# Compact S5 weights in scratch memory, a second rotation table, and a delay before preparation products in the recorded list

## The chip, the cores and the metric

One core of one Trainium2 chip runs the whole program in one launch. The metric is the device time of an execution in microseconds (us). Each of the core's engines follows its own list of instructions in order: PE is TensorE's matmul, PEld its weight load, DVE is VectorE, ACT is ScalarE, POOL is GpSimd, SP is SyncE, which here only issues DMAs. A wait of one instruction holds up everything behind it on its engine.

## The reference, cut to what matters

The reference is eleven stages on 256 tokens of width 1024: gated feed-forward layers, an S5 mixer, three attention mixers, two squared-relu layers and a final norm. The change concerns the first feed-forward layer (`ffn0`), beside which the S5 weights are prepared, and the S5 mixer behind it.

```python
h = h + 0.5 * swiglu(rms_norm(h, g0), w_gate, w_up, w_down)   # ffn0
hn = rms_norm(h, mix_norm)
u = hn @ w_in                                                  # S5
dt = exp(log_dt); lam = exp(a * dt)                            # complex, 64 groups x 64 states
bb = (lam - 1) / a * b
state[t] = lam * state[t - 1] + bb @ u[t]                      # per group of 16 channels
y = real(c @ state) + d * u
g = gelu(y); g = g * sigmoid(g @ w_glu); h = h + g @ w_out
```

## The kernel before, in words

**Lists.** The kernel is recorded as operations with their tiles. A scheduler (`Schedule.run`) plays them with fixed prices and writes one list for each engine. An operation has a class: `HEAD`, `CRIT`, `FILL`, `LATE` and, last, `BACK`, which is taken only when nothing else can run. All of S5's preparation is `BACK`, so it is woven between the work of `ffn0`. The play decides only the order; on the chip each engine runs its list with semaphore waits. DMAs are issued from SP and from ACT in list order, and share eight completion semaphores in turn: a ninth DMA waits on its own engine until the first has landed. Every instruction is emitted at line L519.

**Weights.** A 128x1024 piece `raw` is loaded by SP, rounded by ACT to `whi`, and DVE forms the rest `wlo` (6, 6 and 5 buffers). PE multiplies both with the activations (`xs` or `hid`).

**Start.** `load_x` loads the eight feature tiles of `x` into `h`, the first of them from ACT's queue, and `table` makes ACT load its function table early with a one-column activation on `ident`. PE fills the start with ten products of `ident` with itself.

**Preparation** (`s5_prep`). After a chain of small DVE operations it makes, for each half of the 32 pairs of groups, a table of rotations in one buffer `tb` (`table`), and for each of eight tiles m: input weights (`enter`, DVE, then four ACT copies with a mask into `et`), output weights (`powers`, DVE into `pg`, then two ACT copies into `gz`), and products of `gz` with the input matrix `bz` on PE, which give the short lags (`tile_mats`). Two groups share 128 partitions, so `et`, `gz` and the lags hold zeros where one group's channels meet the other's states. Each part goes by a DMA of its own into the DRAM scratch `s5_dr[m]`, 2688 columns wide; the rotations too.

**S5** (`s5`). `load(m)` brings `s5_dr[m]` back into `mt` (two of four buffers lie in `hid`, the room of ffn0's hidden layer, which is free when ffn0's last product is done). `state(m)` multiplies with `et` on PE, DVE rotates, scans and rotates back, `outy(m)` multiplies with the lags and `gz`, and ACT applies gelu. Products with `w_s5i` (`umm`) and `w_s5g` (`glu`) stand between.

```python
        def load(m):
            mts[m] = mbuf[m % 4]
            D.dma_start(out=mts[m], in_=self.s5_dr[m])
```

Of the kernel before, what the change touches and what calls it, by code (L numbers as in the profile page):

```python
# [15 lines left out]
AF = mybir.ActivationFunctionType  # L16
# [15 lines left out]
MT = 2688  # L32
# [142 lines left out]
class Recorder:  # L175
# [71 lines left out]
    def add(self, calls, cls):  # L247
# [5 lines left out]
        o.lat = 2.0 if o.dma else 0.0  # L253
# [29 lines left out]
class Schedule:  # L283
# [6 lines left out]
    def run(self):  # L290
# [106 lines left out]
        while True:  # L397
# [40 lines left out]
            for what, o in batch:  # L438
# [4 lines left out]
                else:  # L443
# [8 lines left out]
                    for b in succ[o]:  # L452
                        if o.wkind is not None and o.wkind == b.wkind:
                            lat = 0.0
                        elif o.eng == b.eng and (not o.dma or b.dma):
                            lat = o.lat if b.eng in "PD" else self.rec.SAME
                        else:
                            lat = self.rec.CROSS + o.lat
                        b.at = max(b.at, now + lat)
                        left[b] -= 1  # L460
                        if not left[b]:
                            if b.at > now + 1e-9:
                                push(b.at, "wake", b)
                            else:
                                avail_add(b)
# [58 lines left out]
class Net:  # L524
# [351 lines left out]
    def s5_prep(self):  # L876
# [9 lines left out]
        self.s5_dn = keep("s5_dn", [P, KD])  # L886
        self.s5_dr = [self.sb(f"s5_dr{m}", [P, MT], pool="dram") for m in range(KD)]
# [111 lines left out]
        tb = tmp("tb", [P, 2, 16, 64])  # L999
# [43 lines left out]
        mask = tmp("mask", [P, 2])  # L1043
        D.dma_start(out=mask, in_=A["s5_mask"])
        bt = tb.rearrange("p r j c -> p (r j c)")[:, 0:1024].rearrange("p (m r c) -> p m r c", m=KD, r=2)
        lbs = [pb.rearrange("p r j n -> p (r j n)").rearrange("p (m s r c) -> p m s r c", m=2, s=4, r=2), tmp("lb", [P, 2, 4, 2, 64])]
        gzs = [tmp(f"gz{i}", [P, 2, 4, 4, 32]) for i in range(2)]
        ets = [tmp(f"et{i}", [P, 4, 2, P]) for i in range(2)]
        lags = [tmp(f"lag{i}", [P, P]) for i in range(2)]
# [5 lines left out]
        for z in gzs + [bz]:  # L1055
            G.memset(z, 0.0)

        def table(half):

            j0 = 16 * half  # L1060
            G.memset(tb[:, 0, :, 31:32], 1.0)
# [30 lines left out]
        def enter(m):  # L1092
# [6 lines left out]
            tt(V, a[:, 0], a[:, 0], b[:, 1], SUB)  # L1099
            tt(V, a[:, 1], a[:, 1], b[:, 0], ADD)  # L1100
            et = ets[m % 2]
            for g in range(2):
                for r in range(2):
                    S.activation(et[:, :, r, 64 * g:64 * g + 64], a[:, r], AF.Copy, scale=mask[:, g:g + 1])
            S.dma_start(out=self.s5_dr[m][:, 0:1024], in_=et.rearrange("p s r q -> p (s r q)"))

        def powers(m):
# [4 lines left out]
            gz = gzs[m % 2]  # L1112
# [4 lines left out]
            tt(V, pa, pa, pq, SUB)  # L1117
            for g in range(2):
                ps = slice(64 * g, 64 * g + 64)
                S.activation(gz[ps].rearrange("p r s j (g n) -> p (r s j) g n", g=2)[:, :, g, :],  # L1120
                             pa[ps].rearrange("p q j n -> p (q j) n"), AF.Copy)

        def tile_mats(m):
# [5 lines left out]
            gz = gzs[m % 2]  # L1129
            S.dma_start(out=self.s5_dr[m][:, 1024:2048], in_=gz.rearrange("p r s j q -> p (r s j q)"))  # L1130
# [6 lines left out]
            V.scalar_tensor_tensor(p[:, 0:32], i4, self.s5_dn[:, m:m + 1], p[:, 0:32], op0=MUL, op1=ADD)  # L1137
            S.activation(lags[m % 2], p[:, 0:P], AF.Copy)
            S.dma_start(out=self.s5_dr[m][:, 2048:2176], in_=lags[m % 2])
# [10 lines left out]
    def s5(self, ph, nxt):  # L1150
# [7 lines left out]
        def share(shape):  # L1158
# [5 lines left out]
            names = "abc"[:len(shape)]  # L1164
# [10 lines left out]
        for t in zss + m4s:  # L1175
            G.memset(t, 0.0)
# [8 lines left out]

        def scale(m):
# [4 lines left out]
        def state(m):  # L1191
            u, mt = us[m], mts[m]
            et = mt[:, 0:1024].rearrange("p (s r q) -> p s r q", s=4, r=2)
            ps = [self.ps(b)[:, 0:P].rearrange("p (r c) -> p r c", r=2) for b in sbanks]
            with self.r.group(CRIT):
                for ri in range(2):
                    for s in range(4):
                        for j in range(4):
                            a = slice(32 * j, 32 * j + 32)
                            PE.matmul(ps[j][:, ri, :], lhsT=et[a, s, ri, :], rhs=u[a, s, :], start=s == 0, stop=s == 3,  # L1200
# [3 lines left out]
            tab = mt[:, 2176:MT].rearrange("p (e j c) -> p e j c", e=2, j=4)  # L1204
# [10 lines left out]
            for ri in range(2):  # L1215
# [3 lines left out]
                            mt[:, 2176:MT].rearrange("p (e q) -> p e q", e=2).unsqueeze(2).to_broadcast([P, 2, 2, T]), op=MUL)  # L1219
# [5 lines left out]
        def outy(m):  # L1225
            z, u, mt = zss[m % NZ], us[m], mts[m]
            gz = mt[:, 1024:2048].rearrange("p (r s j q) -> p r s j q", r=2, s=4, j=4)
            ps = self.ps(4)[:, 0:T].rearrange("p (s c) -> p s c", s=4)
            with self.r.group(CRIT):
                for d in range(4):  # L1230
                    for j in range(4):
                        a = slice(32 * j, 32 * j + 32)
                        PE.matmul(ps[a, d:4, :], lhsT=mt[a, 2048 + 32 * d:2080 + 32 * d], rhs=u[a, 0:4 - d, :], start=d == 0, stop=False,
# [749 lines left out]
```

## Time and profile before

| | us |
|---|---|
| median of 3 runs | 1579.7 (1579.31 to 1580.79) |
| profiled execution | 1576.88 |
| its span, first to last instruction | 1575.1 |
| PE busy | 1538.8 |
| DVE, ACT, POOL busy | 1177.5, 946.3, 76.2 |

The profiled execution is the one in which all rows were taken; it took 1.8 us beside its span, and 2.8 us less than the median. Busy times of engines overlap, so they don't add up. A busy PE can be a slow PE: the column PEclk gives the granted clock, 1.00 for 2.4 GHz and 0.50 for 1.2 GHz, and a mean between them says how a stretch is divided. The S5 preparation runs from about 45 to 230 us, ffn0 ends and S5 begins at about 218 us, and S5 ends near 340 us.

### The profile page before, as it was taken

The page shows a single profiled execution, that of the slowest core. Times are in us where ns is not written, and L with a number is a line of the kernel's source. Part 1 is how long each engine was busy: PE and PEld are TensorE (multiplying, and loading weights), DVE is VectorE, ACT ScalarE, POOL GpSimd, SP SyncE. Part 2 cuts the span into 40 slices and gives each one's busy share as a digit, 9 for nine tenths or more (in the row PEclk, how much of TensorE's full clock was granted, in tenths as well). Part 3 has the DMA queues.
Part 4 walks back from the last instruction along what each step waited for, and adds up shares of the span by engine and source line. Part 5 has one row for each costly group of instructions (what it writes and reads, how often), then busy time and mean ns, then how long its engine had stood idle before and what let it go on. Part 6 is the DMA issues. An engine that isn't in the chain of part 4 may idle for free.

```text
span 1575.1 us, 28813 instructions
## 1 busy us (share of the span) xinstructions
PE 1538.8 (98%) x11018; PEld 1383.7 (88%) x11018; DVE 1177.5 (75%) x2205; ACT 946.3 (60%) x1800; POOL 76.2 (5%) x111
## 2 busy tenths in 40 slices
PE   8998998999999999999999999999999999999998
PEld 8998887998888888889998888989888888888887
DVE  5997878877777777767878777797876557787663
ACT  6566662466655566645666665565787447688642
POOL 1000000000000000003310000010000002100000
PEclk8999999999999999999999999999999999999999
DMA  7667887356656555655447666632665542356561
GB/s 255 216 195 266 255 307 275 133 187 189 187 185 189 184 185 188 187 163 164 134 161 226 188 186 188 207 116 90 217 203 187 188 143 78 122 178 211 186 189 40
DMA packets 94682, 289.29 MB, mean 184 GB/s; under 512 B 18768, under 2 KB 23760, under 8 KB 93520
## 3 DMA queue, kind: packets, MB, share of 16 engines
q1 hardware_dynamic: 90224, 277.44, 55.6%
q10 hardware_dynamic: 4320, 10.01, 1.7%
q8 instruction: 86, 1.41, 0.4%
q14 instruction: 52, 0.43, 0.1%
HBM read 275.22 MB, written 12.19 MB: 182 GB/s over the span
## 4 chain that ended last, share of the span: by engine, by line
PE 86%; DVE 4%; DMA 4%; issue 2%; ACT 2%; POOL 2%; SPq 1%; ACTq 0%; DVEq 0%; POOLq 0%
PE ps L519 86%; DVE wlo L519 1%; DMA s_dr<-tb 1%; DMA raw<-w_s5i 1%; DMA raw<-w_ffn 1%; POOL rs L519 1%; ACT whi L519 1%; SPq L519 1%; DVE h L519 0%; DMA tb<-s_bt 0%; DMA h<-x 0%; DMA tab<-ab_tab 0%; DVE tA L519 0%; POOL qk L519 0%; DMA pb<-s_l 0%
## 5 line engine op out<-in xcount | busy, mean ns | idle before, releaser
L519 ACT ACTIVATE whi<-raw 128x1024 fp32r<-128x1024 f32 (+3 forms) x520 | 522.8, 1011 | 417.4 <-PE ps L519 324.6
L519 PE MATMUL ps<-xs,whi 128*128 128x512 f32 (+1 forms) x2592 | 737.3, 354 | 11.6 <-ACT xs L519 8.4
L519 DVE TENSOR_TENSOR wlo<-raw,whi 128x1024 fp32r<-128x1024 f32 (+3 forms) x520 | 604.4, 1165 | 192.3 <-PE ps L519 145.2
L519 PE MATMUL ps<-xs,wlo 128*128 128x256 f32 x2080 | 567.7, 282 | 0.0
L519 PEld LDWEIGHTS ps<-xs,whi 128*128 128x128 f32 x2592 | 448.5, 190 | 75.6 <-ACT xs L519 9.1
L519 PE MATMUL ps<-hid,whi 128*128 128x512 f32 (+1 forms) x1248 | 424.0, 388 | 0.0
L519 PEld LDWEIGHTS ps<-xs,wlo 128*128 128x128 f32 x2080 | 394.6, 190 | 10.8
L519 PE MATMUL ps<-hid,wlo 128*128 128x256 f32 x1216 | 332.2, 279 | 0.0
L519 PEld LDWEIGHTS ps<-hid,whi 128*128 128x128 f32 x1248 | 229.0, 187 | 49.2 <-issue 0.4
L519 PEld LDWEIGHTS ps<-hid,wlo 128*128 128x128 f32 x1216 | 228.2, 188 | 4.3
L519 PE MATMUL ps<-whi,xs 128*128 128x256 f32 (+1 forms) x544 | 125.6, 312 | 0.0
L519 PEld LDWEIGHTS ps<-whi,xs 128*128 128x128 f32 x544 | 92.1, 188 | 1.0 <-issue 0.8
L519 PE MATMUL ps<-wlo,xs 128*128 128x256 f32 (+1 forms) x272 | 83.3, 306 | 0.0
L519 PE MATMUL ps<-oT,whi 128*128 128x256 f32 x384 | 69.7, 283 | 0.0
L519 POOL TENSOR_TENSOR r_col<-ms,mhalf 128x2 f32<-128x2 f32 x11 | 11.2, 1021 | 1207.2 <-DVE ms L519 1207.2
L519 DVE TENSOR_TENSOR hid<-hv,hid 128x256 fp32r<-128x256 f32 x88 | 37.1, 424 | 31.1 <-ACT hid L519 31.0
L519 PEld LDWEIGHTS ps<-oT,whi 128*128 128x128 f32 x384 | 58.3, 188 | 1.6 <-issue 1.2
L519 ACT ACTIVATE hid<-hv 128x256 fp32r<-128x256 f32 x88 | 36.2, 413 | 33.1 <-DVE hv L519 32.3
L519 ACT ACTIVATE zr<-zr 128x256 f32<-128x256 f32 x128 | 51.0, 410 | 7.4 <-DVE zr L519 7.4
L519 PE MATMUL ps<-oT,wlo 128*128 128x256 f32 x192 | 53.7, 280 | 0.6 <-DVE wlo L519 0.6
L519 PEld LDWEIGHTS ps<-wlo,xs 128*128 128x128 f32 x272 | 51.2, 188 | 0.1
L519 DVE TENSOR_TENSOR zr<-ps,zr 128x256 f32<-128x256 f32 x64 | 26.7, 422 | 28.0 <-ACT zr L519 27.9
(254 smaller groups left out, 1553.4 us busy)
## 6 DMA issues: line engine op xcount, KB each, us to landing
raw<-w_ffn SPq DMA_DIRECT2D x260, 512.0 KB, 4.1
raw<-w_mlp SPq DMA_DIRECT2D x128, 512.0 KB, 4.3
raw<-w_moba_q SPq DMA_DIRECT2D x32, 384.0 KB, 3.0
raw<-w_ab_in SPq DMA_DIRECT2D x18, 512.0 KB, 4.4
hid<-s_dr SPq DMA_DIRECT2D x4, 1344.0 KB, 8.9
mt<-s_dr SPq DMA_DIRECT2D x4, 1344.0 KB, 6.4
s_dr<-gz ACTq DMA_DIRECT2D x8, 512.0 KB, 6.5
s_dr<-et ACTq DMA_DIRECT2D x8, 512.0 KB, 5.8
```

The source lines that it names most:

```text
L519: getattr(getattr(nc, ename), method)(*[real(x) for x in a], **{n: real(x) for n, x in k.items()})
```

## The change

The scratch drops the zeros: it holds 512 columns of input weights, 512 of output weights, 128 of masked lags and 512 of rotations (1664 in place of 2688). DVE writes the first two straight into one of two tiles `out`; one DMA for each m stores it. S5 gets a step `spread(m)`, four ACT copies that put the zeros back, into `ets` and `gzs`. The preparation products take 64 columns in place of 128. Each half has a rotation buffer of its own. In the scheduler a `BACK` DMA counts as 5 us to land in place of 2, and a `BACK` operation on PE is ready 5 us after an operand from another engine. At the start, the early table activation is gone and ACT issues its three loads of `x` one behind the other.

```diff
-MT = 2688
+MT = 1664
+SLACK = 5.0
...
-        o.lat = 2.0 if o.dma else 0.0
+        o.lat = (5.0 if cls == BACK else 2.0) if o.dma else 0.0
...
+                        if b.eng == "P" and b.cls == BACK and o.eng != "P":
+                            lat += SLACK
...
-        tb = tmp("tb", [P, 2, 16, 64])
+        tbs = [tmp(f"tb{i}", [P, 2, 16, 64]) for i in range(2)]
...
+            tb = tbs[half]
...
-            tt(V, a[:, 0], a[:, 0], b[:, 1], SUB)
-            tt(V, a[:, 1], a[:, 1], b[:, 0], ADD)
-            et = ets[m % 2]
-            for g in range(2):
-                for r in range(2):
-                    S.activation(et[:, :, r, 64 * g:64 * g + 64], a[:, r], AF.Copy, scale=mask[:, g:g + 1])
-            S.dma_start(out=self.s5_dr[m][:, 0:1024], in_=et.rearrange("p s r q -> p (s r q)"))
+            e = outs[m % 2][:, 0:512].rearrange("p (r s c) -> p r s c", r=2, s=4)
+            tt(V, e[:, 0], a[:, 0], b[:, 1], SUB)
+            tt(V, e[:, 1], a[:, 1], b[:, 0], ADD)
...
-            tt(V, pa, pa, pq, SUB)
-            for g in range(2):
-                ps = slice(64 * g, 64 * g + 64)
-                S.activation(gz[ps].rearrange("p r s j (g n) -> p (r s j) g n", g=2)[:, :, g, :],
-                             pa[ps].rearrange("p q j n -> p (q j) n"), AF.Copy)
+            tt(V, outs[m % 2][:, 512:1024].rearrange("p (q j n) -> p q j n", q=8, j=4), pa, pq, SUB)
...
-                        PE.matmul(p[32 * j:32 * j + 32, 0:P], lhsT=bz[:, ri, j, :], rhs=gz[:, ri, :, j, :], start=(ri == 0), stop=(ri == 1),
+                        PE.matmul(p[32 * j:32 * j + 32, 0:64], lhsT=bz[:, ri, j, :], rhs=gz[:, ri, :, j, :], start=(ri == 0), stop=(ri == 1),
...
-            S.activation(lags[m % 2], p[:, 0:P], AF.Copy)
-            S.dma_start(out=self.s5_dr[m][:, 2048:2176], in_=lags[m % 2])
+            for g in range(2):
+                S.activation(o[:, 1024:1152].rearrange("p (d g n) -> p d g n", d=4, g=2)[:, :, g, :],
+                             p[:, 0:64].rearrange("p (d n) -> p d n", d=4), AF.Copy, scale=mask[:, g:g + 1])
+            S.dma_start(out=self.s5_dr[m][:, 0:1152], in_=o)
...
+        def spread(m):
+
+            mt, et, gz = mts[m], ets[m % 2], gzs[m % 2]
+            for g in range(2):
+                S.activation(et[:, :, :, 64 * g:64 * g + 64].rearrange("p r s c -> p (r s) c"),
+                             mt[:, 0:512].rearrange("p (q c) -> p q c", q=8), AF.Copy, scale=self.s5_mask[:, g:g + 1])
+            for g in range(2):
+                ps = slice(64 * g, 64 * g + 64)
+                S.activation(gz[ps].rearrange("p r s j (g n) -> p (r s j) g n", g=2)[:, :, g, :],
+                             mt[ps, 512:1024].rearrange("p (q n) -> p q n", n=16), AF.Copy)
...
+            spread(m)
             state(m)
...
-            self.load_x(0, 1, "S")
-            self.table(AF.Copy, self.ident)
-            for k in (1, 2):
-                self.load_x(k, 2 * k, "S")
+            for k in (0, 1, 2):
+                self.load_x(k, max(k + 1, 2 * k), "S")
```

The emitting line moves from L519 to L522. The first place is the head of ACT's list; before, it begins like this (`gains` are the norms' gains, `tab` the early table activation):

```order
L519 DMA gains_92<-gains 128x88
L519 DMA h_114<-x 128x256
L519 ACT_TABLE_LOAD
L519 ACTIVATE tab_119<-ident_60 128x1
L519 DMA h_114<-x 128x256
L519 DMA h_114<-x 128x512
L519 ACTIVATE whi_132<-raw_107 128x256 x2
L519 ACTIVATE xs_140<-h_114,gains_92 128x256
```

And now the head of the same list:

```order
L522 DMA gains_92<-gains 128x88
L522 DMA h_114<-x 128x256 x2
L522 DMA h_114<-x 128x512
L522 ACT_TABLE_LOAD
L522 ACTIVATE whi_135<-raw_107 128x256 x2
L522 ACTIVATE xs_143<-h_114,gains_92 128x256
```

The second and third load of `x` now stand ahead of the table load, among the first eight DMAs of ACT and SP together, so none of them has to wait for another DMA's semaphore.

The second place is PE's list in ffn0; before, six of the eight products of `gz` with `bz` stand among the gate and up products (`ps<-xs`), the third of them here:

```order
L519 MATMUL ps_1655<-xs_140,wlo_1494 128x256
L519 MATMUL ps_1697<-gz_0_124,bz_143 32x128 x8
L519 MATMUL ps_1655<-xs_140,whi_1497 128x256 x2
L519 MATMUL ps_1655<-xs_140,wlo_1538 128x256
```

In the list of the change the eight preparation products are these, of which the first two stand among the gate and up products, five among ffn0's down products (`ps<-hid`) and the eighth among S5's first products, just ahead of the group that needs the last feature tile of `xs`:

```order
L522 MATMUL ps_1425<-out_0_1404,bz_122 32x64 x8
L522 MATMUL ps_1493<-out_0_1489,bz_122 32x64 x8
L522 MATMUL ps_2219<-out_0_1404,bz_122 32x64 x8
L522 MATMUL ps_2356<-out_0_1489,bz_122 32x64 x8
L522 MATMUL ps_2468<-out_0_1404,bz_122 32x64 x8
L522 MATMUL ps_2580<-out_0_1489,bz_122 32x64 x8
L522 MATMUL ps_2708<-out_0_1404,bz_122 32x64 x8
L522 MATMUL ps_2826<-out_0_1489,bz_122 32x64 x8
```

So six products move behind the gate and up part.

The third place is ACT's list where ffn0's last output tile (`dt`) becomes the last tile of `xs`; before (`s_m` is the scan's factor, `sqk` a square for the norm):

```order
L519 ACTIVATE whi_2812<-raw_2680 128x1024
L519 ACTIVATE dt_2826<-ps_2724 128x256
L519 DMA s_dr_0_2171<-et_0_2337 128x1024
L519 ACTIVATE hid_2816<-s_m_0_839 128x4x63 x2
L519 ACTIVATE whi_2855<-raw_2701 128x1024
L519 ACTIVATE et_0_2418<-tA_1087,mask_651 128x4x64 x2
L519 ACTIVATE xs_140<-h_114,gains_92 128x256
L519 ACTIVATE sqk_2890<-h_114 128x256
```

The same place of the change (`hid<-hid,s_mask` is the input part of `spread(0)`, `hid<-hid 64x32x16` its output part, `r_bc` the norm's factor):

```order
L522 ACTIVATE dt_2754<-ps_2645 128x256
L522 DMA s_dr_0_2038<-out_0_1404 128x1152
L522 ACTIVATE hid_2740<-s_m_0_870 128x4x63 x2
L522 ACTIVATE whi_2785<-raw_2634 128x1024
L522 ACTIVATE hid_2740<-hid_2740,s_mask_640 128x8x64
L522 ACTIVATE xs_143<-h_114,gains_92 128x256
L522 ACTIVATE sqk_2822<-h_114 128x256
L522 ACTIVATE hid_2740<-hid_2740,s_mask_640 128x8x64
L522 ACTIVATE hid_2740<-hid_2740 64x32x16 x2
L522 ACTIVATE whi_2852<-raw_2661 128x1024
L522 ACTIVATE out_0_1489<-ps_2826,s_mask_640 128x4x16 x2
L522 DMA s_dr_0_2071<-out_0_1489 128x1152
```

The masked copies from `tA` are gone from this stretch, and the first half of `spread(0)`, which needs `load(0)`, stands ahead of the last `xs`.

## Rows read from the trace of the kernel before

**Rows 1.** The page: busy us, share of the span and instructions of each engine.
```profile
PE 1538.8 (98%) x11018; PEld 1383.7 (88%) x11018; DVE 1177.5 (75%) x2205; ACT 946.3 (60%) x1800; POOL 76.2 (5%) x111
```

**Rows 2.** Waits of PE: waiter <- what ended it: us in total, times, longest.
```profile
PE ps L519 <- ACT xs L519: 8.4, 3, 4.6
PE ps L519 <- ACT gz L519: 6.9, 3, 5.4
PE ps L519 <- issue: 4.9, 3, 2.0
```

**Rows 3.** Windows: stretch, length; busy of PE, PEld, DVE, ACT, POOL; clock, DMA share, GB/s.
```profile
5.90:10.46 4.56, 0.00 (x0) 0.00 (x0) 0.72 (x3) 1.17 (x4) 0.00 (x0) 0.85 0.94 331
10.46:13.70 3.24, 3.23 (x12) 2.70 (x12) 1.14 (x4) 0.87 (x3) 0.00 (x0) 0.50 1.06 410
14.40:17.00 2.60, 2.60 (x10) 2.36 (x11) 2.57 (x6) 2.49 (x7) 0.00 (x0) 0.50 0.63 251
...
145.90:150.00 4.10, 4.10 (x34) 3.68 (x35) 4.02 (x10) 2.26 (x5) 0.00 (x0) 0.62 0.95 275
...
166.00:218.00 52.00, 52.00 (x309) 44.93 (x308) 41.74 (x72) 33.27 (x60) 0.00 (x0) 1.00 0.83 250
...
227.60:250.00 22.40, 22.33 (x351) 21.09 (x353) 15.29 (x29) 6.84 (x10) 0.70 (x1) 0.85 0.87 350
...
264.60:270.00 5.40, 5.39 (x84) 5.18 (x84) 2.99 (x8) 0.80 (x2) 0.00 (x0) 0.54 0.70 254
```

**Rows 4.** Timeline, start: start us, us, engine, operation, [idle before <-releaser].
```profile
1.66 1.28 ACT L519 ACT_TABLE_LOAD   x1 [1.66 <-PEq L1965]
2.96 0.20 ACT L519 ACTIVATE tab<-ident 128x1 f32<-128x1 f32 x1
7.87 1.38 ACTq L519 DMA_DIRECT2D h<-x  x2
9.29 0.72 ACT L519 ACTIVATE whi<-raw 128x256 fp32r<-128x256 f32 x2 [6.13 <-DMA raw<-w_ffn]
13.84 0.51 ACT L519 ACTIVATE xs<-h,gains 128x256 fp32r<-128x256 f32 x1 [2.51 <-DMA h<-x]
```

**Rows 5.** DMA issues at 0.7–1.2 us, last row 215–300 us: count, KB, us to landing.
```profile
raw<-w_ffn SPq DMA_DIRECT2D x2, 128.0 KB, 2.8
h<-x ACTq DMA_DIRECT2D x1, 128.0 KB, 3.3
...
hid<-s_dr SPq DMA_DIRECT2D x4, 1344.0 KB, 8.9
```

**Rows 6.** Timeline, 131 to 146 us, all engines.
```profile
131.15 0.65 PE L519 MATMUL ps<-gz,bz 128*32 128x128 f32 x16
...
134.44 1.06 ACT L519 ACTIVATE whi<-raw 128x1024 fp32r<-128x1024 f32 x1 [3.47 <-DMA s_dr<-tb]
...
136.32 0.21 DVE L519 TENSOR_TENSOR tA<-tb,e 128x32 f32<-128x32 f32 x1 [6.29 <-POOL tb L519]
...
142.59 0.69 DVE L519 TENSOR_TENSOR pg<-pg,pg 128x512 f32<-128x512 f32 x1
...
145.90 1.08 PE L519 MATMUL ps<-gz,bz 128*32 128x128 f32 x16 [5.39 <-ACT gz L519]
```

**Rows 7.** Groups by shape, 165–305 us (wlo: 166–218): count | busy us, mean ns.
```profile
L519 DVE TENSOR_TENSOR wlo<-raw,whi 128x1024 fp32r<-128x1024 f32 x16 | 19.5, 1218 | 2.0 <-PE ps L519 2.0
...
L519 PE MATMUL ps<-hid 128*32 128x64 f32 x256 | 4.4, 220 | 0.0
```

**Rows 8.** Tile gz: durations of its copies. Tile et: landing of its stores.
```profile
L519 ACT ACTIVATE gz<-pg x16: 613/626/632, 97.2 to 164.8; 64x512 f32<-64x512 f32 x16
...
DMA to landing us min/median/max: 3.7/5.8/9.9
```

**Rows 9.** Timeline, ffn0's end, ACT and PE.
```profile
223.88 0.36 ACT L519 ACTIVATE dt<-ps 128x256 f32<-128x256 f32 x1
...
227.56 1.10 PE L519 MATMUL ps<-xs,whi 128*128 128x256 f32 x2 [3.09 <-ACT xs L519]
```

More of the change, by code (lines that the diff above doesn't have):

```diff
@@ L886, in s5_prep @@
         self.s5_dn = keep("s5_dn", [P, KD])
+        mask = self.s5_mask = keep("s5_mask", [P, 2])
         self.s5_dr = [self.sb(f"s5_dr{m}", [P, MT], pool="dram") for m in range(KD)]
@@ L1041, in s5_prep @@
             square(e4[i + 1], e4[i])
-        mask = tmp("mask", [P, 2])
         D.dma_start(out=mask, in_=A["s5_mask"])
-        bt = tb.rearrange("p r j c -> p (r j c)")[:, 0:1024].rearrange("p (m r c) -> p m r c", m=KD, r=2)
+        bt = tbs[0].rearrange("p r j c -> p (r j c)")[:, 0:1024].rearrange("p (m r c) -> p m r c", m=KD, r=2)
         lbs = [pb.rearrange("p r j n -> p (r j n)").rearrange("p (m s r c) -> p m s r c", m=2, s=4, r=2), tmp("lb", [P, 2, 4, 2, 64])]
-        gzs = [tmp(f"gz{i}", [P, 2, 4, 4, 32]) for i in range(2)]
-        ets = [tmp(f"et{i}", [P, 4, 2, P]) for i in range(2)]
-        lags = [tmp(f"lag{i}", [P, P]) for i in range(2)]
+        outs = [tmp(f"out{i}", [P, 1152]) for i in range(2)]
         bz = tmp("bz", [P, 2, 4, 32])
@@ L1054, in s5_prep @@
             G.tensor_copy(i4[c], self.ident[c, c])
-        for z in gzs + [bz]:
-            G.memset(z, 0.0)
+        G.tensor_tensor(i4[:, 0:16], i4[:, 0:16], i4[:, 16:32], op=ADD)
+        G.memset(bz, 0.0)
         def table(half):
             j0 = 16 * half
+            tb = tbs[half]
             G.memset(tb[:, 0, :, 31:32], 1.0)
@@ L1078, in table @@
             for m in range(4):
-                D.dma_start(out=self.s5_dr[4 * half + m][:, 2176:MT].rearrange("p (r j c) -> p r j c", r=2, j=4),
+                D.dma_start(out=self.s5_dr[4 * half + m][:, 1152:MT].rearrange("p (r j c) -> p r j c", r=2, j=4),
                             in_=tb[:, :, 4 * m:4 * m + 4, :])
@@ L1128, in tile_mats @@
                 S.activation(bz[ps, :, :, g * NN:(g + 1) * NN], bb[ps, :, 4 * m:4 * m + 4, :], AF.Copy)
-            gz = gzs[m % 2]
-            S.dma_start(out=self.s5_dr[m][:, 1024:2048], in_=gz.rearrange("p r s j q -> p (r s j q)"))
+            o = outs[m % 2]
+            gz = o[:, 512:1024].rearrange("p (r s j n) -> p r s j n", r=2, s=4, j=4)
             p = self.ps(5)
@@ L1174, in s5 @@
         sas, svs, sws = two("sa", (2, 2, T)), two("sv", (2, T)), two("sw", (2, T))
-        for t in zss + m4s:
+        ets, gzs = two("et", (2, 4, P)), two("gz", (2, 4, 4, 32))
+        for t in zss + m4s + gzs:
             G.memset(t, 0.0)
@@ L1199, in state @@
                             a = slice(32 * j, 32 * j + 32)
-                            PE.matmul(ps[j][:, ri, :], lhsT=et[a, s, ri, :], rhs=u[a, s, :], start=s == 0, stop=s == 3,
+                            PE.matmul(ps[j][:, ri, :], lhsT=et[a, ri, s, :], rhs=u[a, s, :], start=s == 0, stop=s == 3,
                                       skip_group_check=True)
@@ L1203, in state @@
             S.activation(m4[:, :, 1:64], self.s5_m4[:, 4 * m:4 * m + 4].unsqueeze(2).to_broadcast([P, 4, 63]), AF.Copy)
-            tab = mt[:, 2176:MT].rearrange("p (e j c) -> p e j c", e=2, j=4)
+            tab = mt[:, 1152:MT].rearrange("p (e j c) -> p e j c", e=2, j=4)
             sh = [P, 2, 2, 64]
@@ L1232, in outy @@
                         a = slice(32 * j, 32 * j + 32)
-                        PE.matmul(ps[a, d:4, :], lhsT=mt[a, 2048 + 32 * d:2080 + 32 * d], rhs=u[a, 0:4 - d, :], start=d == 0, stop=False,
+                        PE.matmul(ps[a, d:4, :], lhsT=mt[a, 1024 + 32 * d:1056 + 32 * d], rhs=u[a, 0:4 - d, :], start=d == 0, stop=False,
                                   skip_group_check=True)
```

11 lines of the change are left out of this document (5 added, 6 removed).

## Prediction

> **What bounds the kernel now.** I read the busy times first: PE works 1538.8 of 1575.1 us [rows 1], so only some 36 us of its time is empty, and a change can win little unless it fills part of that or takes work from PE. The waits of PE then say who ends these gaps: `xs` from ACT 8.4 us, `gz` from ACT 6.9, "issue" 4.9 [rows 2]. The windows place them and give the clock. There are four places that this change touches.
>
> The first is the start. From 5.90 to 10.46 us PE does nothing, and the 3.24 us behind it run at clock 0.50 [rows 3]. The timeline shows why: ACT loads its table at 1.66 and runs `tab` at 2.96, and then its queue stands until 7.87, when it issues the next two loads of `x`; only then come `whi` (9.29) and, at 13.84, the second `xs` [rows 4]. Yet the first pieces land 2.8 and the first tile of `x` 3.3 us after issues made before 1.2 us [rows 5]. By the list these two loads are the ninth and tenth DMA of ACT and SP, so ACT waits for the semaphore of an earlier piece, not for its own data.
>
> The second is the up projections, where PE stops 5.39 us at 145.90 for `gz` and runs at a mean clock of 0.62 for 4.10 us behind it. Ahead of this ACT waits 3.47 us for the landing of the rotation table's store, and DVE 6.29 us for POOL's fill of `tb` [rows 6], which waits for the same stores, since there is one buffer.
>
> The third is ffn0's end: `dt` comes at 223.88, some 5.9 us after the last down product (218). PE has other S5 products until 224.47, and those with the last tile of `xs` (k=7) start at 227.56 after 3.09 us [rows 9]; the next 22.4 us have clock 0.85 [rows 3]. The fourth is S5 itself, with the "issue" waits and clock 0.54 at 264.6 to 270 [rows 2, 3].
>
> **The change part by part.** Each estimate is a difference to the profiled execution's 1576.88 us (span 1575.1 and 1.8 beside it), which is 2.8 below the median.
>
> *Start.* One more issue on ACT costs at most 0.69 us (1.38 for two [rows 4]), so two more in front move the table load from 1.66 to at most 3.0 and its end to 4.3. Two `whi` take 0.72, one `xs` 0.51, which gives 5.5 to 5.9, just when the warm-up ends. The 4.56 us go, and so do 0.70 us in which PE waits for the second `xs` (13.70 to 14.40: the first twelve products end there, and that `xs` ends at 14.35 [rows 3, 4]). Running at full clock would give another 1.6 (half of 3.23), but from 14.40 on ACT and DVE are both full, 2.49 and 2.57 of 2.60 us [rows 3], and set the pace whatever the clock, so I count 0.5: **-5.8**. Bounds: -6.9 with all of the clock; -2.5 where the weights' transfer takes the place of the semaphore. For that speaks that the DMA share is already 0.94 and 1.06 in these stretches: the 384 KB of the later loads, now ahead of weights, are 1.2 us at 331 GB/s. PE waits those 1.2, falls to half clock over a stretch as before (1.6), and 2.5 of 5.3 are left. I stay near the other end, because the pieces that PE needs first land by 4 us [rows 5].
>
> The Trainium skill speaks for the lower end ("DMA: Bandwidth & Descriptors", section "Issuing engines are not separate DMA queues"): transfers started by several engines run on the same 16 DMA engines and interleave. By it the loads that ACT issues earlier slow the pieces that SP issued, and the sum would stand 3.3 higher; the DMA share near 1 agrees. The same skill speaks against a table load directly ahead of work ("ScalarE: Activation LUTs", section "What ACT_TABLE_LOAD costs"): 1283 ns and a drain of about 1380. The trace agrees with the first (1.28) and shows no drain: the next activation starts 0.02 us behind it. With the drain the start would win about 1.4 less.
>
> *Up projections.* Two products of `gz` stay, with 5 us more in the list between operand and product; the others go to the down part and S5. The second table no longer waits for the first one's stores, so DVE's 6.29 and ACT's 3.47 go, unless something else is late there. The waits on `gz` total 6.9, the clock gives 1.6 (0.38 of 4.10), together 8.5; I leave 0.6 for a remaining wait: **-7.9**. Bounds: -8.5, and -3 if the two that stay wait like the mean of the three before (6.9/3 = 2.3 each, with clock some 5.5 lost again). ACT has no late store ahead of them, so I stay near the gain.
>
> *Narrower products.* A group of 16 takes 0.65 us at 128 columns [rows 6], 41 ns each; the nearest row at 64 columns has 256 in 4.4 us [rows 7], 17 ns each, 0.28 for 16. Eight times 0.37 is 3.0; I take **-2.5**, since a small group between large products starts and ends no faster. Bounds -3.0 and 0 (a fixed cost).
>
> *Down part.* DVE is busy 41.74 of 52 us [rows 3]. The `powers` of five or six tiles come here, three operations of 0.69 [rows 6]: six times 2.07 is 12.4, which makes 54 of 52. DVE is full, and its `wlo` is what PE waits for next. What hides it is the five `wlo` buffers: 16 pieces in 52 us are 3.25 us each [rows 7], so 16 us of work ahead. It should suffice but for the last stretch: **+1.5**, bounds 0 and +6 (half of the 12.4, if the cover is not full when the work comes). Dropping `et` and `gz` copies takes from ACT two of 0.63 [rows 8] and four of `et` per tile, so it has room here.
>
> *S5's entry.* With the copies gone, `dt` should come earlier. But the list now puts the first half of `spread(0)` ahead of the last `xs`, and that needs `load(0)`, which can start only when `hid` is free. Before, a load of 1344 KB took 8.9 us [rows 5]; 832 KB at the same rate take 5.5. Issued just after 218, when the down products end, it lands at about 224, and a copy of 512 columns takes 0.63 (as `gz` does), so `xs` starts at about 224.7 in place of 227.00 (0.56 ahead of k=7): of the 3.09 us 2.3 go. Of the clock's 3.4 (0.15 of 22.4) I count half, 1.7. Against it stand the norm's factor `r_bc`, now behind the rest of `spread(0)` (1.9 us for three more copies), DVE's backlog, and the eighth preparation product, which now stands ahead of k=7: +1.5. Sum **-2.5**. Bounds: -6.5 (all of both), and +4 (load as slow as before, 8.9 us, so `xs` at 228 and later, and `r_bc` behind it).
>
> *S5 itself.* ACT gets four copies of 0.63 per tile, 20 us for eight, where it is busy 6.84 of 22.4 us [rows 3]. That cover is large, but the order is a chain (load, spread, products, scan), and the copies for the next tile stand ahead of small ones that hold a PSUM bank. The 4.9 us of "issue" and half clock (0.46 of 5.40 is 2.5) are about what can be won or doubled: **-0.5**, bounds ±5.
>
> *DMA bytes.* Two times 1024 columns of 128 rows less for each of eight tiles, 8.4 MB; the queues are not what PE waits for inside ffn0, so 0; the loads of S5 are counted above.
>
> **The sum.** -5.8 - 7.9 - 2.5 + 1.5 - 2.5 - 0.5 = -17.7, so a profile near 1559.2 and a median near **1562**.
>
> **The rivals.** A: the start stays bound by transfers, as its DMA share suggests; against it stands that the data were there at 4 us. The start gives 2.5: 1565.3.
>
> B: DVE's backlog reaches S5's entry. DVE at 54 of 52 speaks for it, the 16 us of cover against. Down part +5, entry +4: the sum is -7.7, and the time 1572.
>
> C, slower: the stores. A tile `out` is written by `enter` and `powers` and comes free when the one store, behind the product and the lags, has landed. Two tiles allow DVE 2 x 8.7 us (52/6) of holding. Powers 2.07, the delay of 5, product and copies 1.5 and a landing of 5.8, at the longest 9.9 [rows 8], make 14 to 18.5, so the wait is about 0.5 per tile at the worst. If ACT's lag, 5.9 us at `dt`, stands in the chain more than once, holding can reach 32: DVE waits (32 - 17.4)/2 = 7.3 for each of six tiles, 44 in all. With 2.2 of overload and less 16 of cover, 30 are left in place of +1.5, and the time is 1590. The whole gain is gone at 19 us left, which is a holding of 28.4.
>
> D: the delay doesn't do what it says; the two products in the up part still wait: 1567.
>
> **How the numbers follow.** My forecast 0.62, A 0.12, B 0.14, C 0.05, D 0.07. Range 1552 to 1573: below by the open gains together (start 1.1, narrow 0.5, entry 4, S5 4.5), above to B, which leaves C and half of B out. About 0.2% (3 us) is what a measurement of this kernel can tell from no change. Forecast, A, D and half of B are faster; the other half of B, in which S5 too loses 5, comes to no change or just over it; C is slower: 0.88, 0.06 and 0.06.
>
> **What would show it.** Start: the first product behind the warm-up at about 6 us, no gap of 4.56. Up part: no wait of some us on `out` (the old `gz`), clock 1.00 at 145 to 150. Narrow groups: 0.3 us for 16. Down part: DVE near 52 of 52 and no wait of PE on `wlo`. Entry: `xs` before 225 and less than 1 us ahead of k=7, shifted by what was won earlier. S5: no longer waits than 2 us. I am wrong if DVE waits for `s_dr` stores, if PE waits for `wlo` or a spread copy, or if the first gap is still there with another name.

## The result and the profile after

The change takes 1557.01 us in the median of four runs (1555.28 to 1557.43), the kernel before 1579.51; the ratio is 0.9858 with a 95% interval of 0.9841 to 0.9875. On another chip (run `after_again`) it was 0.9891 (0.9868 to 0.9914). The forecast was 1562, with 1552 to 1573 as range: the time lies in it, 5 us below the forecast. The profiled execution took 1557.43 us, 1.8 less than the 1559.2 that the sum gave for a profile.

The profiled execution has a span of 1555.6 us, 19.5 less than before. The page gives PE 8.9 us less busy time than [rows 1] at the same number of instructions; the rest is empty time that went.

```profile
PE 1529.9 (98%) x11018; PEld 1376.4 (88%) x11018; DVE 1177.2 (76%) x2205; ACT 946.1 (61%) x1791; POOL 77.4 (5%) x112
```

The waits of PE up to 350 us (engine, tile and line, what ended it: total, times, longest) answer to [rows 2]. `xs` has gone from 8.4 to 1.2 and `gz` is gone; in their place stands one wait of 4.4 for DVE's `hid`.

```profile
PE ps L522 <- DVE hid L522: 4.6, 2, 4.4
PE ps L522 <- issue: 2.4, 2, 2.0
PE ps L522 <- POOL ones L591: 1.4, 1, 1.4
PE ps L522 <- DVE xs L522: 1.2, 2, 0.8
PE ps L522 <- ACT xs L522: 1.2, 2, 0.7
```

The windows (columns as in [rows 3]) show the stretch of the start with PE busy 3.67 of 4.56 us where it had been empty, the up projections without a gap, the down part with DVE 61.12 of 64 us busy and PE still never waiting, the first part of S5's entry at clock 1.00, and then the new gap: PE busy 0.14 of 4.50 us, and 6.10 us at clock 0.51 behind it.

```profile
5.90:10.46 4.56, 3.67 (x26) 3.08 (x25) 3.32 (x8) 3.70 (x9) 0.00 (x0) 1.00 0.98 332
110.00:170.00 60.00, 60.00 (x443) 55.53 (x442) 55.22 (x104) 35.40 (x58) 0.00 (x0) 1.00 0.86 264
136.00:200.00 64.00, 64.00 (x435) 55.30 (x434) 61.12 (x107) 37.76 (x67) 0.00 (x0) 1.00 0.87 268
200.00:214.00 14.00, 13.14 (x121) 12.58 (x119) 9.62 (x17) 7.93 (x16) 3.10 (x6) 1.00 0.91 332
214.00:218.50 4.50, 0.14 (x2) 0.00 (x0) 0.46 (x2) 3.04 (x5) 0.95 (x1) 0.90 0.56 190
218.50:224.60 6.10, 6.08 (x76) 5.97 (x77) 4.43 (x11) 3.04 (x5) 0.00 (x0) 0.51 0.89 355
```

The timeline of the start, beside [rows 4]: three loads issued in 1.42 us, the table at 2.62, `whi` at 3.92, `xs` at 4.77, and PE's first product at 5.65, inside the warm-up.

```profile
1.18 1.42 ACTq L522 DMA_DIRECT2D h<-x  x3
2.62 1.28 ACT L522 ACT_TABLE_LOAD   x1 [2.62 <-issue]
3.92 0.95 ACT L522 ACTIVATE whi<-raw 128x256 fp32r<-128x256 f32 x2
...
4.77 0.49 ACT L522 ACTIVATE xs<-h,gains 128x256 fp32r<-128x256 f32 x1
...
5.65 0.64 PE L522 MATMUL ps<-xs,whi 128*128 128x256 f32 x2
```

What the clock did at the start shows in one window, first before, then after the change (columns as in [rows 3]): half clock there, full clock here. The two rows below it are waits of PE that the start still has; a third, 0.45 us for ACT's `xs`, is at 7.91.

```profile
10.46:19.00 8.54, 7.83 (x32) 7.07 (x33) 5.41 (x13) 5.91 (x16) 0.00 (x0) 0.50 0.88 319
...
10.46:19.00 8.54, 7.64 (x62) 7.43 (x63) 7.88 (x16) 8.39 (x17) 0.00 (x0) 1.00 1.03 412
...
10.53 0.39 PE L522 MATMUL ps<-xs,whi 128*128 128x256 f32 x1 [0.37 <-DVE xs L522]
...
13.05 0.38 PE L522 MATMUL ps<-xs,whi 128*128 128x256 f32 x1 [0.83 <-DVE xs L522]
```

S5's entry, beside [rows 9]. The first copy of `spread(0)` waits 2.48 us for its load, `xs` follows, and PE waits 0.73 ahead of k=7. Then the last store of an `out` tile is issued at 211.18. ACT stands 4.31 us for its landing in front of the second tile's `et`, POOL 4.71 in front of `gz`, and behind ACT's wait come `whi` and `r_bc`, for which DVE waits 5.85 and PE 4.38.

```profile
200.19 0.80 SPq L522 DMA_DIRECT2D hid<-s_dr  x2
...
206.46 0.72 ACT L522 ACTIVATE hid<-hid,s_mask 128x512 f32<-128x512 f32 x1 [2.48 <-DMA hid<-s_dr]
...
207.08 0.49 ACT L522 ACTIVATE xs<-h,gains 128x256 fp32r<-128x256 f32 x1
...
207.63 0.90 PE L522 MATMUL ps<-xs,whi 128*128 128x256 f32 x2 [0.73 <-ACT xs L522]
...
211.18 0.33 ACTq L522 DMA_DIRECT2D s_dr<-out  x1
...
215.46 1.33 ACT L522 ACTIVATE et<-hid,s_mask 128x512 f32<-128x512 f32 x2 [4.31 <-DMA s_dr<-out]
...
215.89 0.95 POOL L522 MEMSET gz<- 128x1024 f32 x1 [4.71 <-DMA s_dr<-out]
...
217.65 0.36 ACT L522 ACTIVATE r_bc<-ps 128x256 f32<-128x256 f32 x1
...
218.04 1.41 DVE L522 TENSOR_TENSOR hid<-ps,r_bc 128x256 f32<-128x256 f32 x4 [5.85 <-ACT r_bc L522]
218.52 3.69 PE L522 MATMUL ps<-hid 32*128 32x64 f32 x64 [4.38 <-DVE hid L522]
```

To see where time came from, I compare when the same product starts. PE's products of one form (with `wlo`) come in a fixed number, so the n-th of them is the same point of the program in every kernel. The table gives its start in the timeline of before, and by how much it starts earlier (us) in the profiles of five kernels, of which the last four are told below.

| product | before | change | start alone | storage alone | storage and start | delays alone |
|---|---|---|---|---|---|---|
| 36th with `xs` | 28.10 | -6.6 | -6.9 | -0.1 | -6.9 | -0.5 |
| 216th with `xs` | 92.89 | -6.6 | -6.9 | -0.1 | -6.9 | -0.5 |
| first with `hid` (down) | 153.86 | -17.7 | -2.4 | -11.1 | -17.9 | -6.0 |
| 353rd with `xs` (S5 begins) | 218.16 | -17.9 | -2.4 | -12.0 | -18.8 | -5.3 |
| 380th (behind k=7) | 234.77 | -22.8 | -3.2 | -14.0 | -19.3 | -7.5 |
| 392nd (behind the norm's factor) | 241.62 | -15.6 | -3.2 | -15.9 | -21.4 | -7.6 |
| 480th (near S5's end) | 337.77 | -19.7 | -3.0 | -14.6 | -19.0 | -4.7 |

So the change wins 6.6 at the start, 11.0 in the up projections, 0.3 in the down part and 4.8 by k=7; it loses 7.1 at the norm's factor and wins 4.0 in the rest of S5. The last two figures differ between executions: in the second profile of the same kernel (`after_again`) the loss is 8.7 and the win 6.3, with the same sum to 0.8 us.

### The profile page after: what moved, and what is told of

Its sections match the earlier page's. It is cut to its first block, busy times and chain, and to the rows that moved or that the text cites. A ratio compares the mean times of both kernels' runs of the same rounds, so it can differ in the third digit from the quotient of the medians.

```text
span 1555.6 us, 28796 instructions
## 1 busy us (share of the span) xinstructions
PE 1529.9 (98%) x11018; PEld 1376.4 (88%) x11018; DVE 1177.2 (76%) x2205; ACT 946.1 (61%) x1791; POOL 77.4 (5%) x112
## 4 chain that ended last, share of the span: by engine, by line
PE 91%; DVE 4%; DMA 2%; POOL 2%; issue 1%; ACT 1%; SPq 0%; ACTq 0%; DVEq 0%; POOLq 0%
PE ps L522 91%; DVE wlo L522 1%; POOL rs L522 1%; DVE hid L522 1%; DVE h L522 0%; DMA hid<-s_dr 0%; DMA tab<-ab_tab 0%; DMA raw<-w_ffn 0%; DMA s_dr<-out 0%; ACT whi L522 0%; POOL rb L522 0%; DMA h<-x 0%; POOL qk L522 0%; DVE sa L522 0%; DVE qk L522 0%
## 5 line engine op out<-in xcount | busy, mean ns | idle before, releaser
L522 ACT ACTIVATE whi<-raw 128x1024 fp32r<-128x1024 f32 (+3 forms) x520 | 523.4, 1011 | 408.8 <-PE ps L522 330.7
L522 DVE TENSOR_TENSOR wlo<-raw,whi 128x1024 fp32r<-128x1024 f32 (+3 forms) x520 | 604.3, 1164 | 185.0 <-PE ps L522 143.6
L522 PE MATMUL ps<-xs,whi 128*128 128x512 f32 (+1 forms) x2592 | 731.7, 352 | 3.9 <-DVE xs L522 2.4
L522 PE MATMUL ps<-xs,wlo 128*128 128x256 f32 x2080 | 565.3, 281 | 0.0
L522 PEld LDWEIGHTS ps<-xs,whi 128*128 128x128 f32 x2592 | 444.2, 188 | 66.6 <-DVE xs L522 4.4
L522 PE MATMUL ps<-hid,whi 128*128 128x512 f32 (+1 forms) x1248 | 423.8, 388 | 0.0
L522 PEld LDWEIGHTS ps<-xs,wlo 128*128 128x128 f32 x2080 | 391.8, 188 | 10.8
L522 PE MATMUL ps<-hid,wlo 128*128 128x256 f32 x1216 | 332.3, 280 | 0.0
L522 PEld LDWEIGHTS ps<-hid,whi 128*128 128x128 f32 x1248 | 228.9, 187 | 48.5
L522 PEld LDWEIGHTS ps<-hid,wlo 128*128 128x128 f32 x1216 | 228.2, 188 | 4.2
L522 PE MATMUL ps<-whi,xs 128*128 128x256 f32 (+1 forms) x544 | 125.6, 312 | 0.0
L522 PEld LDWEIGHTS ps<-whi,xs 128*128 128x128 f32 x544 | 92.1, 188 | 1.0 <-issue 0.8
L522 PE MATMUL ps<-wlo,xs 128*128 128x256 f32 (+1 forms) x272 | 83.3, 306 | 0.0
L522 POOL TENSOR_TENSOR r_col<-ms,mhalf 128x2 f32<-128x2 f32 x11 | 11.8, 1074 | 1193.8 <-DVE ms L522 1193.8
L522 PE MATMUL ps<-oT,whi 128*128 128x256 f32 x384 | 69.7, 283 | 0.0
L522 DVE TENSOR_TENSOR hid<-hv,hid 128x256 fp32r<-128x256 f32 x88 | 37.1, 423 | 31.7 <-ACT hid L522 31.4
L522 PEld LDWEIGHTS ps<-oT,whi 128*128 128x128 f32 x384 | 58.4, 188 | 1.6 <-issue 1.2
L522 ACT ACTIVATE zr<-zr 128x256 f32<-128x256 f32 x128 | 51.0, 410 | 7.4 <-DVE zr L522 7.4
L522 ACT ACTIVATE hid<-hv 128x256 fp32r<-128x256 f32 x88 | 36.1, 412 | 29.9 <-DVE hv L522 29.9
L522 PE MATMUL ps<-oT,wlo 128*128 128x256 f32 x192 | 53.7, 280 | 0.6 <-DVE wlo L522 0.6
L522 PEld LDWEIGHTS ps<-wlo,xs 128*128 128x128 f32 x272 | 51.2, 188 | 0.1
L522 DVE TENSOR_TENSOR zr<-ps,zr 128x256 f32<-128x256 f32 x64 | 26.7, 423 | 28.0 <-ACT zr L522 27.9
```

The source lines that it names most:

```text
L522: getattr(getattr(nc, ename), method)(*[real(x) for x in a], **{n: real(x) for n, x in k.items()})
```

## The experiments

All ratios are to the kernel before, run on the same chip.

| run | median us | before | ratio (95% interval) |
|---|---|---|---|
| e1_start | 1570.84 | 1578.18 | 0.9964 (0.9950 to 0.9978) |
| e3_onetable | 1574.64 | 1578.18 | 0.9992 (0.9976 to 1.0008) |
| e4_nodelay | 1558.75 | 1578.18 | 0.9883 (0.9866 to 0.9899) |
| e7_behind | 1552.69 | 1578.18 | 0.9851 (0.9834 to 0.9868) |
| after_again | 1559.01 | 1576.44 | 0.9891 (0.9868 to 0.9914) |
| e7_again | 1553.72 | 1576.44 | 0.9848 (0.9828 to 0.9869) |
| e8_both | 1551.21 | 1576.44 | 0.9835 (0.9815 to 0.9854) |
| e6_compact | 1563.02 | 1576.44 | 0.9917 (0.9896 to 0.9937) |
| e9_compact_start | 1555.67 | 1580.00 | 0.9842 (0.9825 to 0.9858) |
| e10_compact_start_both | 1552.09 | 1580.00 | 0.9825 (0.9811 to 0.9839) |
| e11_delay | 1572.20 | 1580.00 | 0.9954 (0.9942 to 0.9966) |
| e8_again | 1549.68 | 1580.00 | 0.9812 (0.9796 to 0.9828) |

**The start alone**, on the kernel before:

```diff
-            self.load_x(0, 1, "S")
-            self.table(AF.Copy, self.ident)
-            for k in (1, 2):
-                self.load_x(k, 2 * k, "S")
+            for k in (0, 1, 2):
+                self.load_x(k, max(k + 1, 2 * k), "S")
```

> The kernel before with the start edit alone (three loads of x one behind the other on ACT, no early table activation). Theory: the start is worth what the same matmul moved by between the two profiles, 6.6 us, and nothing later depends on it: about 0.9958 of before, 6 to 7 us less, with the first product at about 5.7 us and the stall of 5.4 us for gz still there. Rival: the transfers moved ahead of the weights, or the stall for gz, take it back further on: less than 3 us gained.

The 36th product starts 6.9 us earlier, as the theory has it, but in the profile 4.5 of them are gone by the first down product, as the rival has it. By the ratio 5.7 us are won in all (3.5 to 7.9), nearer to the theory; the profiled execution was the second slowest of eight. The timeline shows where: PE waits twice for `gz`, 3.72 and 4.23 us, and the second table's first product on DVE starts at 132.76, only 3.56 earlier than in [rows 6]. The preparation keeps much of its own pace, so a PE that is earlier waits longer for it.

```profile
120.86 1.08 PE L519 MATMUL ps<-gz,bz 128*32 128x128 f32 x16 [3.72 <-ACT gz L519]
...
132.76 0.21 DVE L519 TENSOR_TENSOR tA<-tb,e 128x32 f32<-128x32 f32 x1 [5.13 <-POOL tb L519]
...
142.34 1.08 PE L519 MATMUL ps<-gz,bz 128*32 128x128 f32 x16 [4.23 <-ACT gz L519]
```

**One rotation buffer**, on the change:

```diff
-        tbs = [tmp(f"tb{i}", [P, 2, 16, 64]) for i in range(2)]
+        tbs = [tmp("tb", [P, 2, 16, 64])] * 2
```

> The change with a single rotation buffer. Theory: the second buffer removed the stall of 5.4 us, so DVE and ACT wait for the table's stores again for some 3 to 6 us, PE stops behind them and the time is 4 to 8 us above the change (about 0.989 to 0.991 of before). Rival: the delay in the list alone keeps the products out of the way; DVE waits, PE does not, and the time is within 2 us of the change (0.985 to 0.987).

The loss is larger than either expected: 1574.64, all but the whole gain. It isn't where the theory put it, though. PE waits nowhere in the up or down part, and its first down product starts at 136.07, 17.8 us earlier than before and as early as in the change. The list, made with 5 us to land for each store and one buffer, puts three of the preparation products at 230, 240 and 244 us, in S5; `load(0)` is issued only at 207.11, in the middle of S5's first products, ACT waits 11.09 us for it, and PE 9.48 us for what stands behind that. Further on PE waits 2.34 and 2.91 us for `out` at the last two of these products, and from 250 to 265 us its clock is 0.70: the 392nd product with `xs` is still 15.3 us ahead of before, the 480th 0.7. So this run tells what the delays do with one buffer, not what the buffer is worth by itself.

```profile
136.07 0.28 PE L522 MATMUL ps<-hid,wlo 128*128 128x256 f32 x1
...
207.11 0.85 SPq L522 DMA_DIRECT2D hid<-s_dr  x2
...
214.00 1.33 ACT L522 ACTIVATE hid<-hid,s_mask 128x512 f32<-128x512 f32 x2 [11.09 <-DMA hid<-s_dr]
...
219.96 0.80 PE L522 MATMUL ps<-xs,whi 128*128 128x256 f32 x2 [9.48 <-DVE hid L522]
...
243.62 0.66 PE L522 MATMUL ps<-out,bz 128*32 128x64 f32 x16 [2.91 <-DVE out L522]
```

**No delays**, on the change (two buffers stay):

```diff
-SLACK = 5.0
+SLACK = 0.0
...
-        o.lat = (5.0 if cls == BACK else 2.0) if o.dma else 0.0
+        o.lat = 2.0 if o.dma else 0.0
```

> The change without the two delays in the list (SLACK 0, and 2 us to land for every DMA). Theory: the buffer and the compact storage do the work and the delays are spare: products stand earlier on PE, each waits at most 0.5 us, and the time is within 3 us of the change (0.984 to 0.988 of before). Rival: the delays are what keeps PE from waiting for its operands: several waits on out of 2 us and more with half clock behind them, 6 to 12 us above the change (0.990 to 0.993).

The time is that of the change within the intervals. The mechanism is half the rival's. Of the waits of PE between 130 and 260 us the largest sum is 4.4 us for `out`, 3.87 of it in the down part, and by S5's begin (353rd product) this kernel is 10.8 us ahead of before where the change is 17.9. But its entry has no long wait for the norm's factor, and behind that (392nd) it is 14.5 ahead against 15.6. The third preparation product is back in the up part, and the row ahead of it shows what holds it: DVE can write its operand into `out` only when the first store of that tile, issued at 127.10, has landed.

```profile
PE ps L522 <- DVE out L522: 4.4, 2, 3.9
```

```profile
127.10 0.33 ACTq L522 DMA_DIRECT2D s_dr<-out  x1
...
134.33 0.69 DVE L522 TENSOR_TENSOR out<-pg,pg 128x512 f32<-128x512 f32 x1 [1.58 <-DMA s_dr<-out]
...
135.17 0.43 PE L522 MATMUL ps<-out,bz 128*32 128x64 f32 x16 [0.49 <-DVE out L522]
```

**`r_bc` ahead of the second tile's copies**, on the change. Only ACT's list moves: `et<-hid` of the second tile stands behind `whi` and `r_bc`.

```diff
+        rop = [o for o in self.r.ops if o.eng == "S"][-1]
...
+            n0 = len(self.r.ops)
             spread(m)
+            if m == 1:
+                for o in self.r.ops[n0:]:
+                    o.deps.add(rop)
```

> The change with one exchange in ACT's list: the second tile's input copies of spread stand behind r_bc instead of ahead of it. Theory: ACT stands 4.3 us in front of these copies, because they are written where the last out tile lay until its store has landed, and r_bc is late by that; PE's wait of 4.4 us at 218.5 and the half clock behind it (about 3 us in 6) go, and the time falls 4 to 7 us below the change (0.981 to 0.983 of before). Rival: something else is late there, first of all the products of the second tile, whose copies now come later: the wait moves by a few us and the time stays within 2 us of the change.

The wait of 4.4 us at the norm's factor is gone, and the median is 4.3 us below that of the change's first runs, which were on another chip. The profiled execution was the slowest of its four runs, and it shows why: the load of `spread(0)`, issued at 200.06, kept its first copy until 208.67, 2.3 us longer than in the change, and PE waited 3.06 us ahead of k=7. The lists are the same up to there, so that difference is one of executions, not of the exchange.

```profile
200.06 0.80 SPq L522 DMA_DIRECT2D hid<-s_dr  x2
...
208.67 0.72 ACT L522 ACTIVATE hid<-hid,s_mask 128x512 f32<-128x512 f32 x1 [4.82 <-DMA hid<-s_dr]
...
209.84 0.90 PE L522 MATMUL ps<-xs,whi 128*128 128x256 f32 x2 [3.06 <-ACT xs L522]
```

To compare it with the change on one chip, both were run again.

> The change itself once more, beside the next three on one chip. Both theories: about 0.986 of before, with the stall of some 4 us for the norm's factor at S5's entry.

> The exchange of spread's second copies with r_bc once more. Its profile before had lost the stall of 4.4 us but had one of 3.1 us ahead of k=7, where the change had 0.7. Theory: that one comes from the landing of load(0), which differs between executions, so the median here is 3 to 6 us below the change on the same chip. Rival: the exchange moves the wait, and the medians are within 1.5 us.

The exchange is 5.3 us below the change in the median (1553.72 and 1559.01), as the theory has it. In its timeline `r_bc` runs at 216.24, ahead of the landing, and the copy that waits for the store keeps nobody.

```profile
216.24 0.39 ACT L522 ACTIVATE r_bc<-ps 128x256 f32<-128x256 f32 x1 [1.55 <-PE ps L522]
...
217.71 1.33 ACT L522 ACTIVATE et<-hid,s_mask 128x512 f32<-128x512 f32 x2 [1.08 <-DMA s_dr<-out]
```

**Both exchanges**: the last `xs` ahead of `spread(0)` as well.

```diff
+        sop = [o for o in self.r.ops if o.eng == "S" and o.wkind is None][-1]
...
+            if m < 2:
+                for o in self.r.ops[n0:]:
+                    o.deps.add((sop, rop)[m])
```

> The change with r_bc ahead of the second tile's copies and, too, the last tile of xs ahead of the first copies of spread. Theory: both of the waits that I saw at S5's entry go (0.7 to 3.1 us ahead of k=7, 4.4 at the norm's factor with half clock behind it): 5 to 9 us below the change on the same chip, and below the exchange alone. Rival: state(0) needs these first copies, so what k=7 wins is lost in front of the first state products; then it equals the exchange alone within 1.5 us.

> The change with both exchanges at S5's entry once more, beside the three others on one chip. Theory: still 0.982 to 0.985 of before and the fastest of the four, by 0 to 3 us over the storage and start with the same exchanges. Rival: buffer and delays cost more than they bring, and that kernel is faster than this one.

In the timeline of the second run PE no longer waits ahead of k=7 at all, but 1.10 us in front of the first state products: ACT meets the load of `spread(0)` at 208.03, and `r_bc` stands behind these copies. So a part of what k=7 wins is lost again, as the rival says. The median is 7.8 us below the change on one chip and 2.5 below the exchange alone, where the intervals of the two ratios overlap; the second run gives 0.9812. What the second exchange adds to the first is not clear of the noise.

```profile
208.03 1.34 ACT L522 ACTIVATE hid<-hid,s_mask 128x512 f32<-128x512 f32 x2 [2.71 <-DMA hid<-s_dr]
...
212.86 0.38 ACT L522 ACTIVATE r_bc<-ps 128x256 f32<-128x256 f32 x1
...
213.75 2.08 PE L522 MATMUL ps<-hid 32*128 32x64 f32 x64 [1.10 <-DVE hid L522]
```

**The compact storage alone**: the change with the start, the one buffer and the prices of the kernel before (the edits above undone together).

> The compact storage alone: the start as before, one rotation buffer, no delays in the list. Theory: without the second buffer the second table waits for the stores of the first and the preparation ends late, so S5's entry pays: 0 to 4 us below before (0.9975 to 1.000). Rival: fewer copies and DMAs on ACT are what freed the up projections, and the storage alone brings 8 us or more (0.995 or less).

The size is the rival's: 13.4 us in the median, 0.83% by the ratio. Its reason, fewer copies and DMAs on ACT, is not what the trace shows first. The second table still waits for the stores of the first (POOL's wait for `s_dr<-tb` is 94.5 us here, 105.5 before), but PE has no product that needs it: behind the second preparation product, at 106.56, the third stands at 171.82, in the down part. In the kernel before six of the eight stood ahead of the down part. By the code the new tile `out` ties them to the tables: `powers` and `enter` fill the same tile, its one store goes when both and the lags are in, and with two tiles the third `powers` waits for the first store. `enter` reads factors that are loaded into the rotation buffer once the table in it is stored, with one buffer the second table. So the first store of `out` comes only at 157.73 here (142.19 in the change, 172.13 in the change with one buffer), and the third product stands behind it in every kernel with the compact storage. Before, `gz` had a store of its own, ahead of `enter`. No run has the old number of copies and DMAs with such a tile, so what their saving adds is not separated.

```profile
106.56 0.43 PE L522 MATMUL ps<-out,bz 128*32 128x64 f32 x16
...
157.73 0.33 ACTq L522 DMA_DIRECT2D s_dr<-out  x1
...
169.79 0.68 DVE L522 TENSOR_TENSOR out<-pg,pg 128x512 f32<-128x512 f32 x1
...
171.82 0.43 PE L522 MATMUL ps<-out,bz 128*32 128x64 f32 x16
```

**Storage and start**, without buffer and delays:

> The change with one rotation buffer and without the delays: compact storage and the new start alone. The storage alone had brought 13 us, and the change with one buffer but with the delays 4. Theory: the second buffer only makes up for what the delays do to the list, and the two together bring nothing: 6 us below the storage alone, within 3 us of the change (0.986 to 0.990 of before). Rival: the buffer or the delays are worth several us of their own, and this stays 4 us or more above the change (0.992 or more).

0.9842: as fast as the change. Buffer and delays together bring nothing on top of the storage that these runs can tell. The start keeps what it wins here: the first down product is 17.9 us ahead, 6.8 more than with the storage alone.

**The same with both exchanges**, that is, storage and start with the two exchanges:

> The kernel of the run above with the two exchanges at S5's entry (last tile of xs ahead of the first copies of spread, r_bc ahead of the second tile's). Theory: the entry pays the same as on the change, 5 to 8 us below the run above. Rival: the stores of the last tiles come later here, so the loads are what the first state products wait for, and less than 3 us are won.

2.7 us by the ratio, within the rival's bound, and 3.6 in the medians, between the two expectations; the intervals overlap. In the run without exchanges there was no wait for the norm's factor to remove: its last products and stores stand elsewhere. The fastest kernel is the change with both exchanges; its lead over this one, 2 us, is within the intervals.

**The delays alone**, on the kernel before:

> The kernel before with the delays in the list alone (5 us to land for a preparation DMA, 5 us more between operand and preparation product). Theory: the wide storage with three stores and six copies of ACT for each tile is what makes gz late, so the delays alone leave PE waiting for gz, and the time is within 4 us of before. Rival: the delays alone take PE's waits away (6.9 us with half clock behind it): 6 to 9 us below before (0.994 to 0.996).

The rival holds: 7.3 us by the ratio. Of the three waits for `gz`, 6.9 us [rows 2], one of 1.96 is left, and by the first down product 5.5 us are won.

```profile
146.98 0.65 PE L522 MATMUL ps<-gz,bz 128*32 128x128 f32 x16 [1.96 <-ACT gz L522]
```

## Why the prediction was right, and where it was not

**Start.** Right: -6.6 for -5.8, near the bound of -6.9. By the thirteenth product (14.40 before, 7.91 after) 6.5 are won: 4.8 because the first one starts earlier, 1.4 because the first twelve run at full clock, and 0.3 of the 0.70 that PE waited for the second `xs`. So the clock counted more than the 0.5 that I gave it, and the second `xs` less. Behind that, full clock wins 1.3 more, and the waits of 0.37 and 0.83 us for DVE's `xs` take nearly all of it back: there ACT and DVE did set the pace, as worked out. Rival A fell: the weights did not take the semaphore's place, at a DMA share of 0.98; ACT waits 0.93 us for one of them, at 6.73. The Trainium skill ("DMA: Bandwidth & Descriptors", "Issuing engines are not separate DMA queues") says that transfers issued by several engines share the same 16 DMA engines; the 3.3 us that I worked out from rows for that case are not in the measured start. In the kernel before, the same edit keeps 3.0 us of 6.9 in its profile and 5.7 by the ratio, because a PE that is earlier waits there for a late `gz`; on the compact storage it keeps 6.8 up to the down part. So in the change these two terms do add, as my sum has it.

**Up projections.** The size was near, the cause wrong, and this is the step of the prediction that failed: "the second table no longer waits for the first one's stores". PE's stall did go, but not by the buffer. The change with one buffer has its first down product 17.8 us earlier, like the change with two, and the storage alone, with one buffer too, wins the same 11.0 us in this part. What did it stands in the sentence before, "the others go to the down part and S5". Four of the six products that stood in this part leave it, since two stay; they are not six, as the part on the change counts them. The delays alone, with the old storage and one buffer, win half of that. Of the 11.0 the two waits in this part are 6.0, the clock 1.6, and the four products that left and the narrower two 3.0, which the sum had in another place; so waits and clock are near the 7.9. One reading was wrong as well: ACT's wait of 3.47 us does not come from the single buffer. It ends with the issue of a store of `gz`, which reads no table. By the order of issue this is the eighth DMA behind the table's first store, at 125.37, so it has to wait for the same one of the eight semaphores, which a second buffer does not change:

```profile
134.02 0.33 ACTq L519 DMA_DIRECT2D s_dr<-gz  x1
```

On top of the storage, buffer and delays bring nothing (0.9842 without them, 0.9858 and 0.9891 with them). The buffer only makes the delays harmless: without it they push the last products into S5. With one buffer the delays cost 21 us: that kernel is 3.5 us below before with them and 24.3 without, each in medians on its own chip.

**Narrower products.** Mis-sized: a group of 16 went from 0.64 to 0.43 us, 0.21 each and 1.7 for eight, not 2.5. The row of 17 ns a product, from a series of 256, did not carry over to groups of 16; 27 ns are left.

**Down part.** I had +1.5; the measured part is -0.3. DVE was nearly full (61.12 of 64, which is 49.7 of 52 where I had worked out 54), and PE waits for `wlo` nowhere. Rivals B and C stayed out here: DVE never waits for a store of `out`.

**S5's entry.** Two errors of opposite sign. k=7 went as worked out: `xs` followed the load, PE waited 0.73 where I had 0.8, and the clock stayed at 1.00, so 4.8 us are won for the 2.3 and 1.7 that I counted. But of `r_bc` I said that it stands "behind the rest of `spread(0)`" and gave it and two other things 1.5. What it stands behind is the first copy of `spread(1)`, whose tile lies in the room of the preparation's tiles and so waits for the last of their stores. That cost 7.1 us, 4.38 of wait and the rest half clock, and the exchange on ACT's list, which moves nothing else there, shows it by getting 5 us back. It was in the order of ACT's list, one row behind the piece that I read; in the trace of before ACT waits for no store there. A wait of PE behind a spread copy was one of my signs of being wrong, and here it came.

**S5 itself.** -4.0 in place of -0.5, within its bounds, and -6.3 in the second profile, just outside them: the twenty microseconds of copies were hidden, and the "issue" waits went from 4.9 to 2.4.

Together entry and S5 gave -1.7 against -3.0; all that stands ahead of S5 gave -17.9 against -14.7. So the sum missed the profiled execution by 1.8 us only. The other 3.2 of the 5 us between forecast and median come from the 2.8 that I added because the median of before lay above its profile: the change's median lies 0.4 below its own.

**Open:** how much of the storage's gain comes from fewer copies and DMAs rather than from the tile that `enter` and `powers` share, how much of the 4.0 in S5 belongs to smaller loads and how much to the order of its list, and why the preparation in the run with the start alone came only 3.56 us earlier when PE was 6.9 earlier.

## What to carry to other kernels

When several edits aim at one stall, each may remove it alone, and their gains don't add: run each alone before keeping all. When a freed room is used again, ask which store must land before the first write to it, and what stands behind that write on its engine; moving one pair of copies behind its two neighbours was worth 5 us here. When two results share a tile and its store, the next use of the tile waits for the later of them; here that kept four products out of a crowded stretch. A gain at the start is worth only as much as the work that the engine meets next is early too.

## What the runs showed of the hardware

The same load of 832 KB for the first tiles, at the same place of the same list, let the first copy start 6.3 us (change) or 8.6 us (first run of the exchange) after its issue: a difference of 2.3 us between two executions, which is as large as several of the terms above. And the clock: behind the wait of 4.38 us it was 0.51 for 6.10 us, and in the kernel before, behind a wait of 4.57 us at the start, it was 0.50 from 10.46 to 19 us.
